# A weighted sum over experts: output stores on a second DMA queue, and blocks of 40 tokens per partition

## The chip, the cores and the metric

The kernel runs on one core of a Trainium2 chip. The metric is device time in microseconds (us) of one execution. Before the change the median of 7 runs is 709.83 us (709.53 to 710.03). A core has a vector engine (DVE), a scalar engine (ACT), a matrix engine (PE), GpSimd (POOL), a queue engine (SP) that here only issues DMAs, and 16 DMA engines that move data between HBM and the on-chip memory (SBUF, 128 partitions).

## The reference

```python
# expert_outputs: (16, 1024, 8, 512) float32;  combine_weights: (16, 1024, 8) float32
def reference(expert_outputs, combine_weights):
    weights = combine_weights[..., np.newaxis]
    return np.sum(expert_outputs * weights, axis=2).astype(np.float32)
```

For each of 16 x 1024 = 16384 tokens, eight rows of 512 floats (16 KB) are each multiplied by one weight and added to one row of 512 floats (2 KB). The input is 268.4 MB, the weights are 0.5 MB and the output is 33.6 MB. There are two floating-point operations for every four bytes read, so nearly all that the kernel does is move data.

## The kernel before, in words

**Tiling.** A token belongs to one partition, and each of the 128 partitions takes 128 tokens. The first 120 of them are the loop: `GROUPS` = 6 groups of `G` = 20 tokens, two rounds of `R` = 10 tokens to a group, so `ROUNDS` = 12. The last 8 (`TAIL`) are handled one by one. In a group, partition p takes 20 consecutive tokens of HBM, so neighbouring partitions read 320 KB apart.

**Buffers.** `ring` holds ten tokens per partition (160 KB), `acc` holds twenty output rows (one half for even rounds, one for odd rounds), `w_t` holds all the weights, and `w_c` a copy of the weights of two rounds that sits at a fixed place, so that the vector engine's loop can address it.

**Loads.** A round's ten tokens come as three DMAs (`CHUNKS`): 4, 4 and 2 tokens, here called c0, c1 and c2. Each DMA is cut into 128 pieces, one per partition, and spread over the 16 DMA engines: 8 pieces for each engine, of 65,536 B for four tokens and 32,768 B for two. A chunk of round n is issued as soon as the vector engine has finished the tokens of round n - 1 that lie in the same slots (`done` counts finished tokens).

**Stores.** One store per round writes ten output rows per partition (20,480 B for each of 128 partitions, 2.6 MB). `loads_and_stores` issues everything on SP's queue in this order: c0, c1, c2 of round n, then the store of round n - 1 (line 98), then c0 of round n + 1. The store of round n - 1 waits for the same count of finished tokens as c2 of round n. DMAs of one queue are served in the order of their issue. After the loop SP issues eight loads of one token each (line 119), the store of round 11, and four small stores of 4, 2, 1 and 1 tokens (`tail_stores`, line 123).

**Weights.** Two DMAs, issued behind the first chunk, bring the weights: one for the loop, in runs of 20 tokens x 8 weights x 4 B = 640 B, and one for the tail.

**Vector engine.** `terms` runs a loop of 6 iterations, two rounds in each. Before a round it takes three kinds of count: the round's weights are copied (`w_set`), the store that last used this half of `acc` has landed (`stored`), and the chunk has landed (`loaded`). For each token it runs one multiplication (line 203) and seven fused multiply-adds (line 186). The tokens go in pairs, so that two tokens take 16 instructions.

**Scalar engine.** `weights` copies ten tokens' weights into `w_c` for each round (line 145); the copy for round n waits until round n - 2 is finished. After the last copy it makes the 32 diagonal matrices of the tail (line 150), five of them ahead of the matrix engine.

**Matrix engine.** For the eight tail tokens it computes four of the eight terms by multiplying with a diagonal matrix; the vector engine adds the other four and the result in PSUM.

Of the kernel before, what the change touches and what calls it, by code (L numbers as in the profile page):

```python
# [10 lines left out]
def kernel(  # L11
# [14 lines left out]

    nc = tc.nc
    fp32 = mybir.dt.float32  # L30
    mult, add = mybir.AluOpType.mult, mybir.AluOpType.add
# [3 lines left out]
    P = 128  # L35
    R = 10
    G = 2 * R
    T_P = T // P
    GROUPS = T_P // G
    LOOP = GROUPS * G  # L40
    TAIL = T_P - LOOP
    ROUNDS = LOOP // R
# [4 lines left out]
    x = expert_outputs.rearrange("b s e d -> (b s) e d")  # L47
    w = combine_weights.rearrange("b s e -> (b s) e")
    o = out.rearrange("b s d -> (b s) d")
    cut = LOOP * P  # L50
    x_g = x[0:cut].rearrange("(n p g) e d -> n p g e d", p=P, g=G)
    w_g = w[0:cut].rearrange("(n p g) e -> p n g e", p=P, g=G)
    o_g = o[0:cut].rearrange("(n p g) d -> n p g d", p=P, g=G)
    x_t = x[cut:T].rearrange("(p j) e d -> p j e d", j=TAIL)
    w_x = w[cut:T].rearrange("(p j) e -> p j e", j=TAIL)
    o_t = o[cut:T].rearrange("(p j) d -> p j d", j=TAIL)
# [13 lines left out]
    ring = one.tile([P, R, E, D], fp32, name="ring")  # L70
    acc = one.tile([P, G, D], fp32, name="acc")
    w_t = one.tile([P, T_P, E], fp32, name="w_t")
    w_c = one.tile([P, G, E], fp32, name="w_c")
# [8 lines left out]
    stored = [sem(f"stored{h}") for h in range(2)]  # L82
    step = sem("step")
    done = sem("done")
# [6 lines left out]
    def load_of(j):  # L91
        return [k for k, (q, m) in enumerate(tail_loads) if q <= j < q + m][0]

    def loads_and_stores(sync):
        def store(n):
            h = n % 2
            sync.wait_ge(done, (n + 1) * R)
            sync.dma_start(
                out=o_g[n // 2, :, h * R : h * R + R], in_=acc[:, h * R : h * R + R]
            ).then_inc(stored[h], 16)  # L100

        for n in range(ROUNDS):
            for c, (r, m) in enumerate(CHUNKS):
                if n:
                    sync.wait_ge(done, (n - 1) * R + r + m)
                g = n % 2 * R + r
                sync.dma_start(
                    out=ring[:, r : r + m], in_=x_g[n // 2, :, g : g + m]
                ).then_inc(loaded[c], 16)
                if n == 0 and c == 0:  # L110
                    sync.dma_start(
                        out=w_t[:, 0:LOOP].rearrange("p (n g) e -> p n g e", g=G), in_=w_g
                    ).then_inc(w_in, 16)
                    sync.dma_start(out=w_t[:, LOOP:T_P], in_=w_x).then_inc(w_in, 16)
            if n:
                store(n - 1)
        for k, (j, m) in enumerate(tail_loads):
            sync.wait_ge(done, LOOP - R + j + m)
            sync.dma_start(out=ring[:, j : j + m], in_=x_t[:, j : j + m]).then_inc(tail_in[k], 16)
        store(ROUNDS - 1)  # L120
        for j, m in tail_stores:
            sync.wait_ge(done, LOOP + j + m)
            sync.dma_start(out=o_t[:, j : j + m], in_=acc[:, j : j + m]).then_inc(tail_out, 16)
        sync.wait_ge(stored[(ROUNDS - 1) % 2], 16)
        sync.wait_ge(tail_out, 16 * len(tail_stores))

    def identity(gpsimd):
        gpsimd.memset(ident, 0.0).then_inc(id_set, 1)  # L128
        gpsimd.affine_select(  # L129
            out=ident,  # L130
            in_=ident,
            compare_op=mybir.AluOpType.not_equal,
            fill=1.0,
            base=0,
            pattern=[[-1, P]],
            channel_multiplier=1,
        ).wait_op(id_set, 1, "sem-ge").then_inc(id_set, 1)

    def weights(scalar):
        scalar.wait_ge(w_in, 32)  # L140
        for n in range(ROUNDS):
            if n >= 2:
                scalar.wait_ge(done, (n - 1) * R)
            h = n % 2
            scalar.copy(  # L145
                out=w_c[:, h * R : h * R + R], in_=w_t[:, n * R : n * R + R]
            ).then_inc(w_set[h], 1)
        scalar.wait_ge(id_set, 2)
        for k, (j, e) in enumerate(diags):
            i = scalar.mul(out=diag[:, k % DIAGS], in_=ident, mul=w_t[:, LOOP + j, e : e + 1])  # L150
            i.then_inc(diag_set, 1)
            if k >= DIAGS:
                i.wait_op(product, k - DIAGS + 1, "sem-ge")

    def first_terms(tensor):
        came = set()
        for k, (j, e) in enumerate(diags):
            if load_of(j) not in came:
                came.add(load_of(j))
                tensor.wait_ge(tail_in[load_of(j)], 16)  # L160
            tensor.wait_ge(diag_set, k + 1)
            tensor.matmul(  # L162
                ps[:, j],
                lhsT=diag[:, k % DIAGS],
                rhs=ring[:, j, e],
                start=e == 0,
                stop=e == pe_e[j] - 1,
            ).then_inc(product, 1)
# [58 lines left out]
            count(i, j, e)  # L227

    with tc.tile_critical(no_gpsimd_drain=True):  # L229
        loads_and_stores(nc.sync)  # L230
        identity(nc.gpsimd)
        weights(nc.scalar)
        first_terms(nc.tensor)
        terms(nc.vector)

# [29 lines left out]
```

## Time and profile before

| What | Value |
|---|---|
| median of 7 runs | 709.83 us (709.53 to 710.03) |
| the profiled execution's own time | 710.36 us |
| its span, first to last instruction | 708.6 us |
| vector engine busy | 628.1 us (89%) |
| scalar engine busy | 16.6 us (2%) |
| matrix engine busy | 32.6 us (5%) |
| DMA queue q1: 9568 packets, 302.52 MB | 99.2% of the time of 16 engines |
| mean rate of all DMA | 427 GB/s |

The profile describes one execution. Its span is 1.76 us shorter than that execution's time, and that execution lies 0.53 us above the median. "Busy" counts compute instructions alone; issuing a DMA or waiting on a semaphore is not counted. A DMA packet here is one contiguous piece for one partition, moved by one of the 16 DMA engines; 16 more packets of 4 B per DMA tell its semaphore that it has landed. The share of a DMA queue is the time of all its packets over 16 times the span.

### The profile page before, as it was taken

To read this page: it belongs to the slowest core of one execution; us is meant where nothing else is said; L and a number is where in the kernel's file an instruction comes from. 1 tells how busy PE (TensorE), PEld (TensorE's weight loads), DVE (VectorE), ACT (ScalarE), POOL (GpSimd) and SP (SyncE) were. 2 spreads that over 40 slices of the span, in tenths; PEclk is the share of its full clock that TensorE was granted. 3 is DMA by queue.
4 is the path that set the end of the run, shared out by engine and by line. 5 is a ranking of instruction groups with operands and counts; after the bars stand their busy time and mean duration, and the time that the engine had idled before them with its cause. 6 is when DMAs were issued, how large, how long until landed. Compare 5 with 4: busy or idle time off the path is not lost. (4 is left out here: it accounts for less than half of the span.)

```text
span 708.6 us, 1388 instructions
## 1 busy us (share of the span) xinstructions
PE 32.6 (5%) x64; PEld 13.0 (2%) x64; DVE 628.1 (89%) x992; ACT 16.6 (2%) x45; POOL 0.7 (0%) x6
## 2 busy tenths in 40 slices
PE   0000000000000000000000000000000000000674
PEld 0000000000000000000000000000000000000221
DVE  0599999899799799799799799799799799899974
ACT  0000000000000000000000000000000000000230
POOL 0000000000000000000000000000000000000000
PEclk9999999999999999999999999999999999999998
DMA  9999999999999999999999999999999999999996
GB/s 411 388 470 418 414 420 439 459 399 463 422 412 446 425 422 465 433 411 448 418 435 435 451 413 446 425 425 437 451 409 457 418 422 444 451 409 423 429 428 287
DMA packets 9570, 302.53 MB, mean 427 GB/s; under 512 B 1120, under 2 KB 1888, under 8 KB 2272
## 3 DMA queue, kind: packets, MB, share of 16 engines
q1 hardware_dynamic: 9568, 302.52, 99.2%
q14 instruction: 2, 0.02, 0.0%
HBM read 268.96 MB, written 33.55 MB: 427 GB/s over the span
## 5 line engine op out<-in xcount | busy, mean ns | idle before, releaser
L186 DVE SCALAR_TENSOR_TENSOR acc<-ring,w_c,acc 128x512 f32<-128x512 f32 x840 | 561.4, 743 | 0.0
L203 DVE TENSOR_SCALAR acc<-ring,w_c 128x512 f32<-128x512 f32 x120 | 52.5, 479 | 66.5 <-DVEq L172 66.5
L162 PE MATMUL ps<-ring,diag 128*128 128x512 f32 x64 | 32.6, 662 | 667.3 <-DMA ring<-in_expert_outputs_dram 667.3
L162 PEld LDWEIGHTS ps<-ring,diag 128*128 128x128 f32 x64 | 13.0, 211 | 686.1 <-DMA ring<-in_expert_outputs_dram 672.0
L186 DVE SCALAR_TENSOR_TENSOR acc<-ring,w_t,acc 128x512 f32<-128x512 f32 x24 | 17.6, 750 | 0.6
L145 ACT COPY w_c<-w_t 128x80 f32<-128x80 f32 x12 | 3.0, 257 | 557.5 <-DVE acc L186 535.2
L150 ACT ACTIVATE diag<-ident,w_t 128x128 f32<-128x128 f32 x32 | 12.4, 399 | 119.6 <-PE ps L162 119.6
L186 DVE SCALAR_TENSOR_TENSOR acc<-ring,w_t,ps 128x512 f32<-128x512 f32 x8 | 5.9, 744 | 7.8 <-PE ps L162 7.8
L145 ACT ACT_TABLE_LOAD x1 | 1.3, 1283 | 0.9 <-SPq L229 0.9
L129 POOL TENSOR_SCALAR_AFFINE_SELECT ident<-ident 128x128 f32<-128x128 f32 x1 | 0.3, 292 | 0.1
L128 POOL MEMSET ident<- 128x128 f32 x1 | 0.2, 204 | 0.5 <-SPq L229 0.5
L249 POOL MEMSET const-bfloat16-1.0<- 128x1 bf16 x1 | 0.1, 102 | 0.0
L249 POOL MEMSET const-uint8-127<- 128x1 uint8 x1 | 0.1, 102 | 0.0
L249 POOL MEMSET const-float32-0.0<- 128x1 f32 x1 | 0.1, 98 | 0.2 <-issue 0.2
L249 POOL MEMSET const-float32-1.0<- 128x1 f32 x1 | 0.1, 98 | 0.0
## 6 DMA issues: line engine op xcount, KB each, us to landing
ring<-in_expert_outputs_dram SPq DMA_DIRECT2D x12, 4096.0 KB, 33.1
out_dram<-acc SPq DMA_DIRECT2D x12, 2560.0 KB, 38.8
ring<-in_expert_outputs_dram SPq DMA_DIRECT2D x8, 2048.0 KB, 32.5
out_dram<-acc SPq DMA_DIRECT2D x1, 1024.0 KB, 18.6
out_dram<-acc SPq DMA_DIRECT2D x1, 512.0 KB, 8.8
out_dram<-acc SPq DMA_DIRECT2D x2, 256.0 KB, 5.4
w_t<-in_combine_weights_dram SPq DMA_DIRECT2D x1, 480.0 KB, 22.6
ring<-in_expert_outputs_dram SPq DMA_DIRECT2D x24, 33.6
```

The source lines that it names most:

```text
L128: gpsimd.memset(ident, 0.0).then_inc(id_set, 1)
L129: gpsimd.affine_select(out=ident, in_=ident, compare_op=mybir.AluOpType.not_equal, fill=1.0, base=0, pattern=[[-1, P]], channel_multiplier ...
L145: scalar.copy(out=w_c[:, h * R : h * R + R], in_=w_t[:, n * R : n * R + R]).then_inc(w_set[h], 1)
L150: i = scalar.mul(out=diag[:, k % DIAGS], in_=ident, mul=w_t[:, LOOP + j, e : e + 1])
L162: tensor.matmul(ps[:, j], lhsT=diag[:, k % DIAGS], rhs=ring[:, j, e], start=e == 0, stop=e == pe_e[j] - 1,).then_inc(product, 1)
L186: return vector.scalar_tensor_tensor(out=acc[:, g], in0=ring[:, g % R, e], scalar=weight, in1=before, op0=mult, op1=add)
L203: i = vector.tensor_scalar_mul(out=acc[:, g], in0=ring[:, g % R, 0], scalar1=weight)
L249: nc = _bacc.Bacc("TRN2", target_bir_lowering=False, num_devices=1)
```

## The change

The change does two things. First, the stores of rounds 0 to 10 move from SP's queue to the scalar engine's queue. Each stands there ahead of the copy of the weights whose wait it takes over: the copy for round n used to wait until round n - 2 was finished, and now the store of round n - 2 waits for that and the copy follows it. The store of round 10 stands behind the last copy and ahead of the diagonal matrices. The store of round 11 and the four small stores (18 tokens) stay on SP's queue, behind the loads of the tail. Second, partition p takes 40 consecutive tokens instead of 20 in each block, which is walked in two halves `b` of 20. Loop bounds, chunks and buffers stay; HBM addresses change (neighbouring partitions are 640 KB apart in the input and 80 KB in the output, where they were 320 KB and 40 KB), and the loop's weights come in 384 runs of 1280 B instead of 768 of 640 B.

```diff
+    M = 2 * G
...
-    x_g = x[0:cut].rearrange("(n p g) e d -> n p g e d", p=P, g=G)
-    w_g = w[0:cut].rearrange("(n p g) e -> p n g e", p=P, g=G)
-    o_g = o[0:cut].rearrange("(n p g) d -> n p g d", p=P, g=G)
+    x_g = x[0:cut].rearrange("(n p b g) e d -> n b p g e d", p=P, b=2, g=G)
+    w_g = w[0:cut].rearrange("(n p m) e -> p n m e", p=P, m=M)
+    o_g = o[0:cut].rearrange("(n p b g) d -> n b p g d", p=P, b=2, g=G)
...
-    def loads_and_stores(sync):
-        def store(n):
-            h = n % 2
-            sync.wait_ge(done, (n + 1) * R)
-            sync.dma_start(
-                out=o_g[n // 2, :, h * R : h * R + R], in_=acc[:, h * R : h * R + R]
-            ).then_inc(stored[h], 16)
-
+    def store(queue, n):
+        h = n % 2
+        queue.wait_ge(done, (n + 1) * R)
+        queue.dma_start(
+            out=o_g[n // 4, n // 2 % 2, :, h * R : h * R + R], in_=acc[:, h * R : h * R + R]
+        ).then_inc(stored[h], 16)
+
+    def loads_and_last_stores(sync):
         for n in range(ROUNDS):
             for c, (r, m) in enumerate(CHUNKS):
...
                 sync.dma_start(
-                    out=ring[:, r : r + m], in_=x_g[n // 2, :, g : g + m]
+                    out=ring[:, r : r + m], in_=x_g[n // 4, n // 2 % 2, :, g : g + m]
                 ).then_inc(loaded[c], 16)
                 if n == 0 and c == 0:
                     sync.dma_start(
-                        out=w_t[:, 0:LOOP].rearrange("p (n g) e -> p n g e", g=G), in_=w_g
+                        out=w_t[:, 0:LOOP].rearrange("p (n m) e -> p n m e", m=M), in_=w_g
                     ).then_inc(w_in, 16)
...
-            if n:
-                store(n - 1)
...
-        store(ROUNDS - 1)
+        store(sync, ROUNDS - 1)
...
-    def weights(scalar):
+    def weights_and_stores(scalar):
         scalar.wait_ge(w_in, 32)
         for n in range(ROUNDS):
             if n >= 2:
-                scalar.wait_ge(done, (n - 1) * R)
+                store(scalar, n - 2)
             h = n % 2
             scalar.copy(
                 out=w_c[:, h * R : h * R + R], in_=w_t[:, n * R : n * R + R]
             ).then_inc(w_set[h], 1)
+        store(scalar, ROUNDS - 2)
         scalar.wait_ge(id_set, 2)
```

More of the change, by code (lines that the diff above doesn't have):

```diff
@@ L229 @@
     with tc.tile_critical(no_gpsimd_drain=True):
-        loads_and_stores(nc.sync)
+        loads_and_last_stores(nc.sync)
         identity(nc.gpsimd)
-        weights(nc.scalar)
+        weights_and_stores(nc.scalar)
         first_terms(nc.tensor)
```

## The prediction

> **What bounds the kernel now.** I read the page first.
>
> ```profile
> span 708.6 us, 1388 instructions
> PE 32.6 (5%) x64; PEld 13.0 (2%) x64; DVE 628.1 (89%) x992; ACT 16.6 (2%) x45; POOL 0.7 (0%) x6
> ...
> DMA  9999999999999999999999999999999999999996
> ...
> q1 hardware_dynamic: 9568, 302.52, 99.2%
> ```
>
> DVE is busy for 89%, the DMA engines for 99.2%: the bound is the DMA engines. Next the busy time by stretch, for one period of a round in the middle and for the end (columns: stretch, its length, each engine's busy time, PE clock, DMA share, GB/s).
>
> ```profile
> 344.80:399.00 54.20, 0.00 (x0) 0.00 (x0) 50.42 (x80) 0.16 (x1) 0.00 (x0) 1.00 1.01 434
> ...
> 690.00:696.10 6.10, 4.06 (x9) 1.44 (x8) 4.07 (x7) 1.61 (x4) 0.00 (x0) 1.00 1.01 434
> 696.10:702.20 6.10, 3.70 (x8) 1.44 (x8) 4.21 (x6) 0.00 (x0) 0.00 (x0) 1.00 0.92 384
> 702.20:706.80 4.60, 0.00 (x0) 0.00 (x0) 0.80 (x2) 0.00 (x0) 0.00 (x0) 0.50 0.25 98
> ```
>
> In a period of 54.2 us DVE works 50.4 us and waits 3.8; the DMA share is full. Only after 696 do some DMA engines fall idle, and not all at once. The packet records of the trace say why. They run end to end on each engine, at fixed prices: 65,536 B take 2,418 ns (median of 3072), 32,768 B 1,215, 20,480 B of a store 761, 16,384 B 612, 640 B 32 and 256 B 18. That is 27.0 GB/s per engine, for loads and stores alike. A few packets take longer, and they gather on one engine: the 16 landing events of a DMA lie 0.6 us apart in round 0, 3.2 us at 268 us and 5.0 us at the last tail load (691.2 to 696.1). The slowest engine has no gap from its first packet at 1.97 us to its last end at 706.76: **704.8 us of service, which with 1.97 ahead and 1.8 behind is the span.** At medians (less 3.5 ns of recorded overlap at each packet's end) its packets would be 698.4. It carries 6.4 us of excess: 0.75 in its first packet, 1.28 beside two fetches of instructions (at 51.3 and 679.4 us), and some 4.4 scattered, most of it in the last packets of c2 before a store (0.3 at 156, 0.4 at 210, 1.0 at 264). The mean engine carries 2.7 in all.
>
> Then DVE's waits and the round's events in order of time.
>
> ```profile
> DVE acc L203 <- DVEq L172: 66.5, 11, 25.1
> DVE acc L186 <- PE ps L162: 7.8, 4, 4.1
> ```
>
> ```profile
> 288.75 0.33 SPq L107 DMA_DIRECT2D ring<-in_expert_outputs_dram  x1
> 288.76 0.26 ACT L145 COPY w_c<-w_t 128x80 f32<-128x80 f32 x1 [54.44 <-DVE acc L186]
> 289.13 0.43 SPq L98 DMA_DIRECT2D out_dram<-acc  x1
> 293.78 0.88 DVE L203 TENSOR_SCALAR acc<-ring,w_c 128x512 f32<-128x512 f32 x2 [5.05 <-DVEq L172]
> ...
> 344.23 0.26 ACT L145 COPY w_c<-w_t 128x80 f32<-128x80 f32 x1 [55.21 <-DVE acc L186]
> 344.60 0.43 SPq L98 DMA_DIRECT2D out_dram<-acc  x1
> ```
>
> Of 66.5 us, 25.1 are the start and the rest is some 4 us a round, always before c0: the store issued ahead of that chunk is served first. The store issued at 289.13 lands at 328.9, behind c0, c1 and c2.
>
> **The change part by part.** The sum is made against the profiled execution (span 708.6, 710.36 with the 1.76 around it); the median is 0.53 lower.
>
> Weights: each engine now serves 48 packets of 640 B x 32 ns = 1.54 us. From 256 B (18 ns) to 640 B (32 ns) a byte costs 0.0365 ns, so 1280 B cost 55.3 and 24 of them 1.33 us. That is -0.2 us on every engine, and on the path, because no engine has a gap.
>
> Stores of rounds 0 to 10 leave SP's queue: 11 DMAs, 88 packets x 761 ns = 67 us on each engine. They run on the same 16 engines, from the same semaphore count and at the same moment (0.4 us earlier: SP issues c2 before the store, ACT does not). The work on an engine is the same; its order is not. At 289 the engines are in c0. Before, the store came after c2. After, it is served among c1's packets, or before c1. So c1 and c2 land up to 8 x 0.761 = 6.1 us later, and c0 of the next round at its old time. DVE has 20.1 us of work in c0 (4 multiplications x 0.479 + 28 multiply-adds x 0.743 = 22.7 at the rows' means; 20.1 by the timeline, since neighbours overlap); c1 comes 19.4 + 6.1 = 25.5 after c0: a wait of about 5 us at c1 in place of about 4 at c0. DVE's wait moves, its sum stays near 41 us. Do the DMA engines then run dry? When a chunk is issued, it lands 33 us later and itself takes 19.4, so 14 us of work stand ahead of it: DVE may be late by 14 before an engine idles, and it is late by 6 at most. 0 us.
>
> Does ACT delay anybody? Behind each store stands a copy of weights, now 0.43 us later (the price of the issue at 289.13). DVE takes it a round later, some 50 us. The last store stands ahead of the diagonal matrices; they move from 562 to 617, and the first product starts at 661: cover of 44 us, and PE is served from five made in advance in 2 us. SP loses 11 issues of 0.43, with nothing behind them that is due. DVE waits for `stored` a period after the issue; the store landed 39 us after it and now lands sooner. The tail loads are issued on DVE's progress, which shifts by 6 us at most, and they land 30 us after their issue. 0 us for all.
>
> Unknown one: what an engine pays for switching between two queues, which the trace of before never shows. If it alternates packet by packet, each store brings 16 boundaries of load and store where it had 2: 14 more x 11 = 154 per engine. The nearest row is such a boundary within one queue: in most rounds the packets at it take their medians (761, 2,418), so 0. Above: all scattered excess of the mean engine, 2.7 - 0.75 = 1.9 us over 11 stores, is 0.17 per store with two boundaries; eight times that, less what is there, is 1.2 x 11 = 13 us. Below: from 16,384 to 32,768 B a packet grows by 1,215 - 612 = 603 ns, which leaves 612 - 603 = 9 ns that do not depend on its size; if a second queue hid them at 88 store packets and as many neighbours, 176 x 9 = -1.6 us. I take 0, the median's row.
>
> The Trainium skill ("DMA: Bandwidth & Descriptors", Queues, rings and completion order) says an engine goes round its queues by packets of about 9 to 17 descriptors, which would be one whole DMA's share of 8 pieces and its semaphore write. By that there would be no more boundaries than before and this term would be 0 again; the trace of before, with one queue, can't show it.
>
> Unknown two: new HBM addresses. 4.4 us of scattered excess can go (-4.4) or come again (+4.4). The tail's loads are the nearest row: its partitions lie 128 KB apart, and its packets take 612 ns against 2,418 / 4 = 604 by the largest ones, 8 ns more and that the fixed part: no penalty. I take 0.
>
> The same page (Latency and other measured facts) speaks against the change: copies with rows 512 KiB apart ran at 207 GB/s per direction, against 214 when the distance was padded. 640 KiB is no power of two, but if it paid those 3%, the loop's loads (192 x 2.418 + 96 x 1.215 = 581 us on an engine) would take 20 us more, an estimate from that page, and the time would be near 730; the tail's row says 0.
>
> **Sum:** 710.36 - 0.2 + 0 + 0 = 710.2 for a profiled execution, **709.6 as the median.**
>
> **The rivals.**
> 1. Faster, the slowest engine catches up. Its scattered 4.4 us grew just before stores in one queue; with another order and other addresses it can lose them. All gone: 705.2; half: 707.4. For: the lag delays the last tail load and the last stores alike, so all of it counts. Against: the two fetches (1.28) stay, and nothing says which of order and address made the rest. 0.32, with the hidden fixed part (708.0) in it.
> 2. Slower, switching queues costs. Place: each boundary on each engine while a store and a chunk are both queued. It decides from 1.42 us / 154 = 9 ns per boundary. Prices 1.4 to 13 us, taken near 4: 713.6, at most 723. For: the long packets of before sit near stores. Against: most boundaries cost nothing. 0.26, with recurring address conflicts (+4.4, 714) in it.
> 3. Slower, DVE becomes the bound: if the store stood ahead of c1 in every round, 50.4 + 5.3 = 55.7 per round against 54.5 is +1.2 x 10 = 12, 721. Against: the DMA then runs ahead, c0 lands before DVE asks, and the store comes behind c1 in the next round. 0.06.
> 4. The stores are moved and nothing else follows: my forecast, 0.36.
>
> **How the numbers follow.** 0.2% is 1.42 us, about what a measurement of this kernel can tell from no change. Within it: 0.36 (own range 708.4 to 711.0). Faster 0.32, slower 0.32. The range reaches down to the whole scattered excess gone (705.2) and up to 716; less than 1 in 10 lies on each side.
>
> **What would show it.** Right: a second queue with 11 x 2.6 MB (9.5% of the engines' time) beside the first, sum 99%; stores landing in some 15 to 30 us in place of 38.7; DVE's waits again near 66 us; 434 GB/s in the middle; 1280-B runs. Wrong: longer packets or under 430 GB/s in the middle (rival 2), DVE over 93% busy with DMA gaps (rival 3), a last tail load landing 2 us or more before 696 with the engines closer together (rival 1).

## The result and the profile after

The changed kernel takes 707.83 us in the median (707.4 to 708.33, 15 runs) against 709.84 (35 runs): a ratio of 0.9972, 95% interval 0.9965 to 0.9979, or 2.0 us less. The forecast was 709.6, no change beyond noise, with a range of 705.2 to 716. The time is in the range, but it lies below the 708.4 at which the case "no change" ended: what happened is the first rival, at about half of its price. The range holds because it was drawn wide enough for that rival; the forecast itself, no change, did not come.

The page after, in the lines that answer to those shown of before:

```profile
span 706.1 us, 1388 instructions
PE 31.0 (4%) x64; PEld 12.2 (2%) x64; DVE 628.1 (89%) x992; ACT 16.7 (2%) x45; POOL 0.7 (0%) x6
...
DMA  9999999999999999999999999999999999999997
...
q1 hardware_dynamic: 7600, 273.68, 89.9%
q10 hardware_dynamic: 1584, 28.84, 9.5%
...
out_dram<-acc ACTq DMA_DIRECT2D x11, 2560.0 KB, 26.5
```

The second queue is there with 9.5% of the engines' time, the sum of the two is 99.4%, and a store lands 26.5 us after its issue in place of 38.8. The bound is the same. The line of before for the stores:

```profile
out_dram<-acc SPq DMA_DIRECT2D x12, 2560.0 KB, 38.8
```

DVE's waits after, and one round in order of time:

```profile
DVE acc L204 <- DVEq L173: 68.3, 13, 25.1
DVE acc L187 <- PE ps L163: 3.5, 2, 1.8
```

```profile
237.98 0.36 ACTq L99 DMA_DIRECT2D out_dram<-acc  x1
238.38 0.26 ACT L145 COPY w_c<-w_t 128x80 f32<-128x80 f32 x1 [54.20 <-DVE acc L187]
238.66 9.36 DVE L187 SCALAR_TENSOR_TENSOR acc<-ring,w_c,acc 128x512 f32<-128x512 f32 x14
...
262.10 0.88 DVE L204 TENSOR_SCALAR acc<-ring,w_c 128x512 f32<-128x512 f32 x2 [4.02 <-DVEq L173]
```

The wait of 4 us has moved from the start of a round (5.05 and 4.18 us there, at 293.78 and 348.38, before) to its second chunk (c1, after the two pairs of tokens of c0, at 262.10), and the sum went from 66.5 to 68.3 us. Moving it bought nothing.

The gain stands in the last stretch. The windows are laid at the landing of the last tail load, 693.6 us here and 696.1 before; columns as in the prediction.

```profile
687.50:693.60 6.10, 3.78 (x9) 1.44 (x8) 4.28 (x7) 1.61 (x4) 0.00 (x0) 1.00 1.01 432
693.60:699.70 6.10, 3.70 (x8) 1.44 (x8) 4.18 (x6) 0.00 (x0) 0.00 (x0) 0.98 0.95 404
699.70:704.30 4.60, 0.00 (x0) 0.00 (x0) 0.77 (x2) 0.00 (x0) 0.00 (x0) 0.50 0.57 227
```

The same three stretches come 2.5 us earlier, and in the last one the engines are busy for 57% where they were for 25%: they finish closer together. The 16 landing events of the last tail load lie 2.2 us apart (691.4 to 693.6) in place of 5.0 (691.2 to 696.1). The fastest engine gained nothing; the slowest came forward by 2.5 us, and it is the one that sets the end. Its last packet ends at 704.22 in place of 706.76.

How far the engines are apart accounts for the times of the profiled executions, here and in the experiments below. The profiled execution's time less the spread of the last tail load is 710.36 - 4.96 = 705.4 us before and 707.86 - 2.18 = 705.7 after; over eleven of the thirteen profiles it lies between 705.3 and 705.9, while the times themselves range over 2.5 us. The two others are kernels below that change something else: one changes the end, one runs the engines dry once.

The packet records show where the excess went. Counted are packets over 60 ns above the median that their size has after (65,536 B: 2,418 ns, 32,768 B: 1,213, 20,480 B: 761), from 112 to 660 us, where the first store and the fetches of instructions don't fall: **before 50 such packets with 8.8 us of excess over all engines, after none.** Of the 8.8 us, 5.8 are in packets of c2, ahead of a store, 1.9 in the store's own and 1.1 in the 65,536 B packets behind it. Not every store has them: before, none stands beside the store whose pieces run from 482 to 491 us. The medians are nearly the same in both: 2,418 ns for 65,536 B, 1,215 and 1,213 for 32,768 B, 761 for a store's 20,480 B.

### The profile page after: what moved, and what is told of

Read it like the earlier page. It is cut to its first block, busy times and chain, and to the rows that moved or that the text cites. A ratio compares the mean times of both kernels' runs of the same rounds, so it can differ in the third digit from the quotient of the medians.

```text
span 706.1 us, 1388 instructions
## 1 busy us (share of the span) xinstructions
PE 31.0 (4%) x64; PEld 12.2 (2%) x64; DVE 628.1 (89%) x992; ACT 16.7 (2%) x45; POOL 0.7 (0%) x6
## 5 line engine op out<-in xcount | busy, mean ns | idle before, releaser
L204 DVE TENSOR_SCALAR acc<-ring,w_c 128x512 f32<-128x512 f32 x120 | 52.6, 480 | 68.3 <-DVEq L173 68.3
L163 PE MATMUL ps<-ring,diag 128*128 128x512 f32 x64 | 31.0, 632 | 666.3 <-DMA ring<-in_expert_outputs_dram 666.3
## 6 DMA issues: line engine op xcount, KB each, us to landing
out_dram<-acc ACTq DMA_DIRECT2D x11, 2560.0 KB, 26.5
```

The costliest lines, as they stand in the source:

```text
L163: tensor.matmul(ps[:, j], lhsT=diag[:, k % DIAGS], rhs=ring[:, j, e], start=e == 0, stop=e == pe_e[j] - 1,).then_inc(product, 1)
L204: i = vector.tensor_scalar_mul(out=acc[:, g], in0=ring[:, g % R, 0], scalar1=weight)
```

## The experiments

The change has two halves, and it was open which of them removed the long packets. Theory Q says the queue, theory A the addresses. In the middle of the kernel (110 to 650 us) before, after and the two halves all move 432 to 434 GB/s; what differs is how far the engines are apart at the end.

**The queue alone**

```diff
 # the changed kernel, but with before's blocks:
-    x_g = x[0:cut].rearrange("(n p b g) e d -> n b p g e d", p=P, b=2, g=G)
-    w_g = w[0:cut].rearrange("(n p m) e -> p n m e", p=P, m=M)
-    o_g = o[0:cut].rearrange("(n p b g) d -> n b p g d", p=P, b=2, g=G)
+    x_g = x[0:cut].rearrange("(n p g) e d -> n p g e d", p=P, g=G)
+    w_g = w[0:cut].rearrange("(n p g) e -> p n g e", p=P, g=G)
+    o_g = o[0:cut].rearrange("(n p g) d -> n p g d", p=P, g=G)
...
```

> Stores of rounds 0 to 10 on the scalar engine's queue, but blocks of 20 tokens and weights in 640-byte runs as before. Theory Q (the long packets around each store, which piled up on one DMA engine, come from the store standing in one queue with the loads): nearly all of the gain stays, 707.9 to 708.2 us (0.2 given back for the weights), landing events of the last tail load about 2.2 us apart, no long packets after 100 us but the two beside the fetches of instructions. Theory A (the new HBM addresses removed them): about 709.6 to 709.9, 5 us apart, long packets near each store.

Measured: 708.61 us (707.74 to 708.93), ratio 0.9980 (0.9971 to 0.9989). No long packets after 112 us: theory Q holds on that. But the last tail load's events lie 3.2 us apart, not 2.2, and 0.8 us were given back where 0.2 were expected.

```profile
688.20:694.30 6.10, 5.23 (x11) 1.85 (x9) 4.15 (x7) 2.01 (x5) 0.00 (x0) 0.91 1.02 438
694.30:700.40 6.10, 3.70 (x8) 1.44 (x8) 4.42 (x6) 0.00 (x0) 0.00 (x0) 1.00 0.98 413
700.40:705.00 4.60, 0.00 (x0) 0.00 (x0) 0.80 (x2) 0.00 (x0) 0.00 (x0) 0.78 0.36 140
```

The last load lands at 694.3, between 693.6 after and 696.1 before, and the share in the last stretch (36%) lies between too.

**The blocks alone**

```diff
 # before, with the views of the change and all stores on SP's queue:
-    x_g = x[0:cut].rearrange("(n p g) e d -> n p g e d", p=P, g=G)
-    w_g = w[0:cut].rearrange("(n p g) e -> p n g e", p=P, g=G)
-    o_g = o[0:cut].rearrange("(n p g) d -> n p g d", p=P, g=G)
+    x_g = x[0:cut].rearrange("(n p b g) e d -> n b p g e d", p=P, b=2, g=G)
+    w_g = w[0:cut].rearrange("(n p m) e -> p n m e", p=P, m=M)
+    o_g = o[0:cut].rearrange("(n p b g) d -> n b p g d", p=P, b=2, g=G)
...
```

> Blocks of 40 tokens and weights in 1280-byte runs, all stores on SP's queue as before. Theory Q: only the 0.2 us of the weights, 709.5 to 709.8, last tail load about 5 us apart, and long packets in the last loads before a store. Theory A: 707.7 to 708.2 and about 2.2 us apart.

Measured: 709.98 us (709.67 to 710.32), ratio 1.0004 (0.9995 to 1.0013): nothing gained, not even the 0.2 of the weights. 58 long packets with 8.5 us of excess, about as many as before, and the last tail load's events lie 4.2 us apart.

```profile
689.60:695.70 6.10, 3.79 (x9) 1.44 (x8) 4.06 (x6) 1.60 (x4) 0.00 (x0) 1.00 1.02 438
695.70:701.80 6.10, 3.70 (x8) 1.44 (x8) 4.20 (x6) 0.00 (x0) 0.00 (x0) 1.00 0.95 400
701.80:706.40 4.60, 0.00 (x0) 0.00 (x0) 0.76 (x2) 0.00 (x0) 0.00 (x0) 0.69 0.31 122
```

The new addresses by themselves do not remove the long packets. Theory A falls.

**One queue, the store ahead of c2**

```diff
+                if n and c == C - 1:
+                    store(n - 1)
                 if n:
                     sync.wait_ge(done, (n - 1) * R + r + m)
...
-            if n:
-                store(n - 1)
```

> One queue as before and blocks of 20, but SP issues the store of round n - 1 ahead of c2 of round n and not behind it (both wait for the same count). Theory Q: the long packets move to the last packets of c1, 65,536 B, in front of the store; the time stays within 0.2% of before, 709 to 711, spread of the last tail load 4 to 6 us. A rival, theory O (it is only the place of the store behind the short chunk c2 that costs): the long packets go, 707.8 to 708.4, spread near 2.2 us.

Measured: 709.69 us (709.49 to 710.22), ratio 0.9999 (0.9990 to 1.0008), last tail load 4.0 us apart, 41 long packets with 6.5 us. Half of the excess, 3.2 us in 15 packets, is now in the 65,536 B packets of c1, ahead of the store (363.5 us: 794 ns over, 307.3: 310); 2.2 us in 15 packets are in c2, now behind the store, and 1.0 in the stores. So it is not the place behind the short chunk c2, it is the neighbourhood of a store in one queue with the loads.

**The store of round 11 on the second queue as well**

```diff
-        store(sync, ROUNDS - 1)
...
             if k >= DIAGS:
                 i.wait_op(product, k - DIAGS + 1, "sem-ge")
+            if k == 15:
+                store(scalar, ROUNDS - 1)
```

> The changed kernel with the store of round 11 also on the scalar engine's queue, between the diagonal matrices of the tail, in place of SP's queue behind the last load. Work-conserving engines finish the stores no earlier, but the last tail loads share the engines with the store's 8 x 0.761 = 6.1 us: if the engines alternate packet by packet, the last tail load lands up to 6.1 us later (near 699.5 in place of 693.6), then PE 3.7 + DVE 3.0 + about 4.5 to the end of the last store: 710.5 to 713 us. If the tail load is not delayed (the store done before the last loads come), 707.8.

Measured: 711.95 us (711.81 to 712.15), ratio 1.0031 (1.0019 to 1.0043): slower than before, as worked out. The chain that ended last, in order of time (start, length, what):

```profile
663.47 36.20 DMA ring<-in_expert_outputs_dram
699.67 0.04 issue
699.72 3.71 PE ps L164 x8
703.43 0.02 issue
703.45 0.76 DVE acc L188
```

and the same piece of the changed kernel:

```profile
663.41 30.20 DMA ring<-in_expert_outputs_dram
693.61 0.04 issue
693.65 3.71 PE ps L163 x8
697.37 0.03 issue
697.39 0.76 DVE acc L187
```

The last tail load lands 6.06 us later, which is the store's 8 x 0.761 = 6.1 on the engine. Two thirds of that reach the end: the last small store, with no large store ahead of it any more, lands 2.0 us after its issue in place of 4.0. While work is to be had in the loop, another order of the packets cost nothing (store ahead of c2, 0.9999); at the end, what goes ahead of the last load delays it by its full length. Leaving the store of round 11 behind the loads is worth 4.1 us (711.95 against 707.83).

**The same two kernels again, and the parts of the blocks**

The next four ran side by side. Their kernel before took 709.49 us in the median, 0.3 less than beside the other runs, so they are best compared with each other.

> The changed kernel again, beside the next three on one chip: 707.6 to 708.1 us.

Measured: 707.87 us (707.44 to 708.2), ratio 0.9977 (0.9968 to 0.9986).

> The queue alone again (blocks of 20). In its first run it stood at 708.61, 0.8 above the changed kernel, though 0.2 are all that the packets of the weights explain. Theory N (what is left is where the first store happens to put the slow engine, which varies from run to run): 707.9 to 708.7, scattered over 1 us. Theory B (the blocks themselves bring 0.6 us more through their HBM addresses): 708.4 to 708.8 and no run under 708.2.

Measured: 708.41 us (707.84 to 709.41), ratio 0.9984 (0.9975 to 0.9993). Theory B is out in the form given (four of 11 runs lie under 708.2), and the scatter over 1.6 us speaks for N; still the median is 0.5 above the change's, and it was 0.8 above in the first run.

```diff
 # the changed kernel, weights in 640-byte runs:
-    w_g = w[0:cut].rearrange("(n p m) e -> p n m e", p=P, m=M)
+    w_g = w[0:cut].rearrange("(n p b g) e -> b p n g e", p=P, b=2, g=G)
...
+                    for b in range(2):
                         sync.dma_start(
-                            out=w_t[:, 0:LOOP].rearrange("p (n m) e -> p n m e", m=M), in_=w_g
+                            out=w_t[:, 0:LOOP].rearrange("p (n b g) e -> b p n g e", b=2, g=G)[b],
+                            in_=w_g[b],
                         ).then_inc(w_in, 16)
...
```

> The changed kernel with blocks of 40 tokens, but the loop's weights fetched in runs of 640 bytes (two DMAs of 384 pieces). By packets: 48 x 32 = 1.54 us per engine against 24 x 55 = 1.32, and 16 more semaphore writes of 9 ns on one each: 0.23 us more than the changed kernel, 708.0 to 708.2. If the weights' runs carry the 0.8 us between the queue alone and the whole change: 708.5 to 708.7.

Measured: 707.98 us (707.32 to 708.62), 0.1 over the change where 0.23 were expected; with the scatter of these runs the two agree. So by the medians the runs of the weights do not carry the 0.5 to 0.8 us.

```diff
 # the changed kernel, blocks of 120 tokens:
-    x_g = x[0:cut].rearrange("(n p b g) e d -> n b p g e d", p=P, b=2, g=G)
-    w_g = w[0:cut].rearrange("(n p m) e -> p n m e", p=P, m=M)
-    o_g = o[0:cut].rearrange("(n p b g) d -> n b p g d", p=P, b=2, g=G)
+    x_g = x[0:cut].rearrange("(p b g) e d -> b p g e d", p=P, g=G)
+    w_g = w[0:cut].rearrange("(p m) e -> p m e", p=P)
+    o_g = o[0:cut].rearrange("(p b g) d -> b p g d", p=P, g=G)
...
```

> The changed kernel with blocks of 120 tokens per partition (neighbouring partitions 1920 KB apart in the input) and weights in runs of 3840 bytes. By packets: 8 of about 150 ns = 1.2 us per engine against 1.32: 0.1 us less, 707.6 to 707.9. If longer blocks help through their addresses (theory B), under 707.4; if far apart partitions get in each other's way, over 708.5 with packets of 65,536 B longer than 2,418 ns in the middle.

Measured: 707.89 us (707.69 to 708.19), the same as the change. Longer blocks bring nothing more and cost nothing.

One thing in the profiles of these runs is worth a note, though it settles nothing. In every kernel with a second queue but the next one the slowest engine's lag (the spread of c0's landing events) is fixed by the time that c0 of round 2 has landed (128 to 130 us) and then stays within 0.2 us, until a fetch of instructions near 680 us adds 1.0. That lag is 2.1, 2.6 and 2.2 us in the three profiles with 640-byte runs (queue alone twice, and the one above) and 1.1 to 1.6 in the profiled runs with longer ones. So the lag of one profiled run goes with the runs of the weights, but the medians don't bear it out: 0.1 us for the runs by themselves, 0.4 for the addresses (708.41 against 707.98), both inside a scatter of 1.3 us and more. What of the 0.5 to 0.8 us belongs to which stays open.

**c2 beside the store on the second queue**

```diff
...
         scalar.wait_ge(w_in, 32)
+        load(scalar, 0, C - 1)
         for n in range(ROUNDS):
             if n >= 2:
+                scalar.wait_ge(done, (n - 1) * R)
+                load(scalar, n - 1, C - 1)
                 store(scalar, n - 2)
...
+        scalar.wait_ge(done, (ROUNDS - 1) * R)
+        load(scalar, ROUNDS - 1, C - 1)
         store(scalar, ROUNDS - 2)
```

Here SP issues c0 and c1 alone, and `load` is the DMA of one chunk.

> The changed kernel with the load of c2 moved to the scalar engine's queue too, directly ahead of the store of the round before it, which waits for the same count. SP's queue keeps c0 and c1. Theory Q1 (a store behind a load in one queue makes the last pieces of that load long): long packets of 32,768 B come back in the rounds after 110 us, they pile up on single engines, last tail load 3.5 to 5 us apart, 708.7 to 710 us. Theory Q2 (packets get long only where a store must take its place in the one queue that feeds the engine; with a second queue at work nothing is seen): no long packets after 110 us but the two beside the fetches, 2 to 2.5 us apart, 707.6 to 708.3.

Measured: 709.30 us (709.21 to 709.35), ratio 0.9993 (0.9984 to 1.0002). The time is where Q1 put it, for another reason. There are no long packets between 112 and 660 us, and the last tail load's events lie 1.06 us apart, closer than in any other kernel: as to the packets, that is Q2. So a load that stands directly ahead of a store in one queue is not enough to make long packets, when another queue has loads as well. The time went at one place:

```profile
72.00:73.40 1.40, 0.00 (x0) 0.00 (x0) 1.40 (x4) 0.00 (x0) 0.00 (x0) 1.00 1.28 421
73.40:76.00 2.60, 0.00 (x0) 0.00 (x0) 2.60 (x5) 0.00 (x0) 0.00 (x0) 1.00 0.48 176
```

A packet is counted in the window in which it starts, so the share here only shows that starts stop and come again. The packet records show the engines empty for 1.5 us on average before 73.3 us: with c2 on the other queue the short first rounds ran out of issued loads (c0 of round 1 is issued at 72.33, when 15 of the 16 engines had finished all that they had). On 14 engines the first packet behind that gap took some 0.7 us longer, as the first packet of the kernel does; over all 16 that is 0.6 us on average. Together that is 2.1 us, and without it the kernel would stand near 707.2, an estimate that leaves the engines as close together as the gap itself brought them (the events of the next c0 lie 0.2 us apart). The gap healed less than it cost: the time is 1.5 us above the changed kernel's.

**A small store at the start**

```diff
...
     def weights_and_stores(scalar):
+        scalar.wait_ge(id_set, 2)
+        scalar.dma_start(out=o_t[:, TAIL - 1, 0:P], in_=ident).then_inc(early, 16)
         scalar.wait_ge(w_in, 32)
...
         store(sync, ROUNDS - 1)
+        sync.wait_ge(early, 16)
```

> The changed kernel with one small extra store (128 x 512 B into rows that the last store overwrites) on the scalar engine's queue at the start of the kernel. In the changed kernel two packets of each engine were 0.2 to 1.0 us longer at 76 to 82 us, just ahead of the first store. Theory W (a price paid once, at the first store on a queue, whatever its size): these long packets go from 76 to 82 and some appear near 3 us; time the same or up to 0.7 us less, 707.1 to 707.9. Theory F (they belong to the first full-size store): they stay at 76 to 82, and 8 packets of about 30 ns are added, 707.8 to 708.2.

Measured: 708.16 us (707.48 to 708.89), ratio 0.9977 (0.9968 to 0.9986). The eight 512-byte packets of 27 ns an engine went out from 7.3 us on with nothing long beside them, and the long packets at 74 to 84 us stayed: 0.81 us per engine, 0.72 in the changed kernel. Theory W falls; the price belongs to the first full-size store.

**Stores in two halves**

```diff
-        queue.dma_start(
-            out=o_g[n // 4, n // 2 % 2, :, h * R : h * R + R], in_=acc[:, h * R : h * R + R]
-        ).then_inc(stored[h], 16)
+        for r in range(h * R, h * R + R, R // 2):
+            queue.dma_start(
+                out=o_g[n // 4, n // 2 % 2, :, r : r + R // 2], in_=acc[:, r : r + R // 2]
+            ).then_inc(stored[h], 16)
...
```

The counts that are waited for on `stored` double as well.

> The changed kernel with each store of rounds 0 to 11 cut in two of five rows (10,240 B per packet). 12 x 8 = 96 more packets per engine and as many more boundaries between the queues. If a packet has about 9 ns that do not depend on its size and a change of queue is free: 96 x 9 + 12 x 9 = +1.0 us, 708.7 to 709.0. If a change of queue costs 20 ns or more by itself, over 710.5. If a second queue hides the fixed part of a packet: 707.7 to 708.1.

Measured: 708.12 us (707.66 to 708.5), ratio 0.9975 (0.9965 to 0.9985): 0.3 over the change, at the upper bound of the last case (708.1) and well below the first. Half a store takes 385 ns where half of 761 is 380.5, so the record says 4.5 ns more a half, 9 a pair; but at each packet's end the records overlap by 3 to 4 ns, and the sum of 96 packets comes to 96 x (9 - 3.5) = 0.5 us. A change of queue that costs 20 ns or more is excluded: the eleven stores on the second queue bring 88 more pieces, and 88 such changes would be 1.8 us.

## Why the prediction was right in part and wrong in its centre

**Right: the bound, and what hides what.** The DMA engines were the bound and stayed so (99.2%, 99.4%), without a gap in the loop. DVE's wait moved from c0 to c1, "about 5 us at c1 in place of about 4 at c0" (measured 4.0: on an engine six of a store's eight pieces are served before c1 has landed and two among c2's, where the sum took up to all eight before c1), its sum "near 41" (68.3 - 25.1 = 43.2). ACT's issues delayed nobody: 0.36 us each, and the copies follow at once. The tail's matrices, 0 us: DVE waits 3.5 us for PE, less than the 7.8 before.

**Right: the weights.** 384 packets of 1,280 B take 55 ns each, 55.3 foreseen. As a time the 0.2 us are too small for these runs to confirm.

**Right: unknown one.** The engines do alternate piece by piece. The packet records of the store issued at 237.98 show it on nearly every engine: after three pieces of c1 the store's and c1's come in turn, six of the store's before c1 has landed, then the last two in turn with pieces of c2. So a store lands after 26.5 us though its own pieces take 6.1. There are 16 boundaries per store, and they cost nothing: the medians are 2,418 and 761 ns as before. The second rival (a price for each switch) is out; the halved stores bound it further. The Trainium skill ("DMA: Bandwidth & Descriptors", Queues, rings and completion order) has an engine drain a whole packet of about 9 to 17 descriptors from one queue before it switches. The records above show single pieces of 20,480 to 65,536 B, and those of the halved stores single ones of 10,240 B; the measurement decides.

**Right: unknown two, as far as the row distance goes.** The input's partitions lie 640 KB apart, in one experiment 1920 KB, and 65,536 B still take 2,418 ns. The 20 us that the prediction estimated from the same page's figure for rows 512 KiB apart (Latency and other measured facts) did not come; no run here has that distance itself.

**Wrong: the step that takes the slowest engine's scattered excess as given.** The sum took 0 for it under "new HBM addresses" (ends -4.4 and +4.4), and rival 1 had it fall. It fell by 2.3 us: the service of the slowest engine went from 704.8 to 702.3 (704.22 - 1.95), and 0.2 of these 2.5 us are the weights. Two things failed there. First, the size: at 0.32 rival 1 stood behind "no change" at 0.36, though the row in hand showed excess in the last packets before stores and the change took the stores from that place. Second, the sum filed the cause under the addresses, with only the fixed 9 ns per packet under the queue (rival 1 left open which it was). The runs show the reverse: with a store in the loads' queue there are 41 to 58 long packets whatever the blocks (before, blocks alone, store ahead of c2), with the loop's stores on a second queue there are none, in all ten profiles of eight kernels. That the queue removes them is shown. What makes packets near a store long was not shown: half of the excess or more stands ahead of the store (in c2 before, in c1 when the store came ahead of c2), but with c2 ahead of the store on the second queue there were none, and no run here takes the mechanism apart. Nor is the whole gain shown to be the queue's: it gives 1.1 to 1.2 of the 2.0 us by itself, the blocks by themselves give nothing, and the rest, 0.5 to 0.8 us that come only with both, stays open.

**What stays of the lag.** Rival 1's "all gone" would have been 705.2. As it said, the two fetches of instructions stay (51.4 and 681.2 us, each with one packet 0.66 us longer), and the first store still costs each engine 0.7 us.

**The measured gain is smaller than the profiles' difference**: 2.0 us by medians, 2.5 by spans, because the profiled execution of before lay 0.5 above its median and that of after did not.

## What to carry to other kernels

When the 16 DMA engines run without a gap, as here, the slowest of them sets the time (in eleven profiles 705.3 to 705.9 us plus the spread of the last load), so look at how far apart the landing events of one DMA are and at where the distance grows; the mean share (99.2%) hides it. Moving stores to a second queue removed the long packets beside them and was worth 1.1 to 1.2 us of 710 here by itself, not because the stores land sooner (the vector engine waited 68.3 us in all where it had waited 66.5); a changed order cost nothing while work was queued, and at the end a store of 6.1 us that shared the engines with the last loads cost 4.1, so the last stores belong behind the last loads. These are effects of 0.2 and 0.6%: they need runs of both kernels side by side, and a repeat of any half of a change that seems to gain 0.5 us.

## What was not expected of the hardware

- Around the first full-size store the load packets ahead of its first pieces and between them get longer on every engine, by 0.7 us per engine in sum in the changed kernel (76 to 82 us) and 0.7 before (mostly at 98 to 102 us, in the last packets of c2); the other profiles have 0.4 to 1.1. A small store at the start does not take it away. Later stores on a second queue cost nothing of the kind.
- With the loop's weights in 768 runs of 640 B, one of SP's issues of the loop's loads takes 13.8 to 14.8 us; with longer runs none of them takes more than 0.53. It is hidden here, since SP's next issue is due at 45 us. The view of the loads' lines, first before, then after (shortest, median, longest issue in ns):

```profile
L107 SPq DMA_DIRECT2D ring<-in_expert_outputs_dram x36: 327/328/14532, 1.0 to 617.0; - x36
```

```profile
L109 SPq DMA_DIRECT2D ring<-in_expert_outputs_dram x36: 327/328/532, 0.9 to 619.1; - x36
```

- After the one idle gap seen, of 1.5 us on average, the first 65,536 B packet of 14 engines takes some 0.7 us longer, as it does at the start of the kernel (0.3 to 0.9 us before).
